# Issuing the attention scores of two heads together, alternating between the halves of the array's rows

## The chip, the cores and the metric

One core of a Trainium2 chip runs the whole program. The metric is the device time of one execution in microseconds (us); the median over several executions counts. The engines named below are PE (TensorE, the matrix products; its weight loads are listed apart as PEld), DVE (VectorE), ACT (ScalarE), POOL (GpSimd) and SP (SyncE, which issues the transfers).

## The reference

A backbone of two layers over 1024 latent tokens on a grid of 16 x 64 and 256 context tokens, 1024 channels, all in float32. The change lies in the neighbourhood attention of the first layer: 8 heads of 64 channels. A latent token attends to a window of 8 x 16 grid neighbours and to all context tokens; a context token attends to the context alone.

```python
s_nb = jnp.einsum('bchd,bicjhd->bhcij', q_row, k_nb) * scale + jnp.transpose(bias, (0, 2, 1, 3))
s_cx = jnp.einsum('bchd,bnhd->bhcn', q_row, k_ctx) * scale
p = jax.nn.softmax(jnp.concatenate([s_nb.reshape(n_b, n_h, GRID_W, n_win), s_cx], axis=-1), axis=-1)
...
return jnp.einsum('bhcij,bicjhd->bchd', p_nb, v_nb) + jnp.einsum('bhcn,bnhd->bchd', p[..., n_win:], v_ctx)
```

## The kernel before

The program runs through the layers in turn: projections of layer 0, then a stage in which attention and the mLSTM heads are made together, the output product, the MLP, and layer 1 (RWKV-7 and its MLP). The change touches only the stage of attention and mLSTM.

Heads lie in pairs: head 0 of a pair has its 64 channels on partitions 0 to 63 of the tiles q and k, head 1 on partitions 64 to 127. A product that contracts over 64 partitions uses the half of the array's rows that these partitions feed; the profile writes its form as 64\*128. The generator `attn_tiles` yields 80 tiles: for each of 4 pairs, for each of 10 blocks j of 128 queries (8 latent blocks, 2 context blocks), one tile for head 0 and then one for head 1. A tile with a neighbourhood has two score products: `s2`, against 256 context keys, and `s1`, against 384 neighbourhood keys (256 in the blocks at the left and right edge). A tile of a context block has `s2` alone. Each float32 product shows as two passes in the trace: 80 `s2` are 160 MATMUL records.

`attention` works on a tile in three steps, some tiles in flight. `first` issues the scores (L798, L803), takes the row minimum of `s2` on DVE (L799; q is negated), adds the bias to `s1` and takes the minimum on DVE (L804), then exponentials on ACT (L806 reads `s2`, L808). `second`, LA = 2 tiles later, transposes the probabilities on PE (L819, `ptr`) and copies them out on ACT or, each third time, DVE (L826, L824). `third`, one tile later, multiplies with the values (L836, `po`). Every product goes into one of 8 PSUM banks that the whole program shares under one tag (`kk.bank`); a bank comes back when its last reader is done.

`weave` advances four generators in turn: per attention tile two steps of the mLSTM heads (L667 `pc`, L683 and L685 `pa`, read by DVE L670 and L688 and ACT L687; at a head's start L646 `st` and L655 `kt`), 0.9 step of the modulation vectors (L151 `ada`, whose weights `araw` of 512 KB come by transfer), and now and then a load. A scheduler then sets each engine's order from this program order and gives out the banks; each engine runs its list in order. The SP list is one such list too, so a transfer waits for the ones ahead of it.

Of the kernel before, what the change touches and what calls it, by code (L numbers as in the profile page):

```python
# [33 lines left out]
def behind(gen, n):  # L34
    """The items of gen, each only after n more have come."""
    q = []
    for x in gen:
        q.append(x)
        if len(q) > n:
            yield q.pop(0)  # L40
    yield from q


def weave(*gens):
    """Advance (generator, steps per round, rounds of delay) in turn until all are done."""
    live = [[g, n, -n * d] for g, n, d in gens]
    while live:
        for e in list(live):
            e[2] += e[1]
            while e[2] >= 1:  # L50
                e[2] -= 1
                try:
                    next(e[0])
                except StopIteration:
                    live.remove(e)
                    break


class K:
    """Pools: W weights, S slabs, T small tiles, ps PSUM, cst constants, dram scratch."""  # L60
# [36 lines left out]
    def load_w(self, src, kt, n, eng=None, rows=128):  # L97
        """src [rows, kt, n] in DRAM -> exact parts (hi, lo), [rows, kt, n]."""
# [5 lines left out]
    def mmk(self, outs, w, x, cks, first, last):  # L104
        """One contraction tile of a product in three passes: outs[i] += w.T x over the chunks; w, x: (hi, lo)."""
# [12 lines left out]
def joint(kk, ws, xs, cks, name):  # L118
    """Products over the same operands (a list or a generator), by contraction tiles: banks of each."""
    ps = [[kk.bank(name) for _ in cks] for _ in ws]  # L120
    for k, x in enumerate(xs):
        for p, w in zip(ps, ws):
            kk.mmk(p, (w[0][:, k, :], w[1][:, k, :]), x, cks, k == 0, k == KC - 1)
    return ps


def ada_steps(kk, l, ada_w, blocks, raw, sb, ahead=1):
    """Modulation vectors of layer l, one block of 512 in five steps.  raw(): tile [128, 1024] for weights, loaded ahead; sb(): [128, 512]."""
# [14 lines left out]
    for i, (nb, q) in enumerate(todo):  # L143
# [19 lines left out]
        if nb in (2, 3, 8, 9):  # L163
            nc.vector.tensor_scalar(m, m, 1.0, None, ALU.add)      # parts 1 and 4 are kept as 1 + scale
# [3 lines left out]
def ada_w(kk, l, w, blocks, tags=("araw",)):  # L168
    """The same, with tiles of pool W."""
# [9 lines left out]
class Stats:  # L179
    """1 / rms over the channels of 8 slabs [128, n] that come one by one.  The tokens lie in 4 groups of n / 4, a quadrant of  # L180
    partitions each."""
# [14 lines left out]
    def rstd(self):  # L196
        """The result on all partitions: slab [128, n]."""
# [19 lines left out]
def norm_mod(kk, xt, n, mods, part, hs, segs, rstd):  # L217
    """Modulated rms norm, as exact parts hs[c] = (hi, lo); parts part (shift), part + 1 (1 + scale)."""
# [13 lines left out]
def mlp(kk, xt, n, hs, w1, w2, gate, segs, side=None, done=None):  # L232
    """xt += gate * relu(h w1)^2 w2, in place.  w1 [32, 128, 8, 128], w2 [32, 128, 1, 1024].  side: generator advanced along the way;
    done(c): called as xt[c] is complete."""
# [19 lines left out]
    def square(f):  # L254
        """relu(h w1)^2 as exact parts, a chunk a step."""
# [64 lines left out]
def out_proj(kk, w, rows, xt, n, mods, part, segs, ww):  # L320
    """xt += gate * (cat w), in place; ww: the weights of the first tiles, made together from the rows of cat as they come."""
# [33 lines left out]
NA = 12      # blocks of modulation vectors made beside attention and mLSTM  # L355
HD, AD = 9, 20
LA = 2
# [10 lines left out]
def proj_tokens(kk, hs, w, n, cb, tiles, rows):  # L368
    """Token-major products: cb(t, psum [128, n]) for each token tile.  w: (hi, lo) [128, 4, n] for each half of k."""
# [14 lines left out]
def mlstm_rows(kk, psg, I):  # L384
    """Gates -> quantities of each token, direction and head.  On partitions (direction, 16 chunks of which 10 are used, head): the
    tokens of a chunk; the running maximum passes from chunk to chunk on a second layout, partitions (direction, head).  A generator,
    then kk.mcols: M in DRAM [128, 128] and columns [128 t, 5, 2, 16, 4]: g, M_start - M_t, -m_t, g - M_end, M_start - M_end
    (exponentials but for g)."""
# [23 lines left out]
    # log sigmoid(f) = min(f, 0) - log1p(e), e = exp(-|f|); log1p(e) = 2 atanh(s), s = e / (2 + e)  # L412
# [94 lines left out]
def project0(kk, I, hs, dr, early):  # L507
    """Projections of layer 0, left in DRAM: qk (mLSTM, roped, channel-major), vb, sig(o), q and k (neighbourhood, channel-major,
    (column block, row, column) order), va (token-major, same order)."""
# [37 lines left out]
    # neighbourhood q, k by head pairs  # L547
# [71 lines left out]
def mlstm_head(kk, h, dr, cat):  # L619
    """One head, both directions; leaves the gated, normed output channel-major in DRAM."""  # L620
# [112 lines left out]
def attn_tiles(kk, I, dr):  # L733
    """The attention tiles: (start, finish stages) in order."""
# [50 lines left out]
def attention(kk, tiles):  # L785
    """Neighbourhood and context attention, some tiles in flight."""
# [3 lines left out]
    def first(tile):  # L790
        (q, knb, kcx, bias, vt), cell, x = tile[:3]         # q is negated: the scores come out as -s
# [5 lines left out]
        s2 = kk.bank("s2")  # L797
        nc.tensor.matmul(s2[:, 0:256], q, kcx, start=True, stop=True)  # L798
        V.tensor_reduce(m[:, 0:1], s2[:, 0:256], AX.X, ALU.min)  # L799
        mm = m[:, 0:1]  # L800
        if nb:
            s1 = kk.bank("s1")
            nc.tensor.matmul(s1[:, 0:nb], q, knb, start=True, stop=True)  # L803
            V.tensor_tensor_reduce(p[:, 0:nb], s1[:, 0:nb], bias, 1.0, m[:, 0:1], ALU.add, ALU.min, m[:, 1:2])  # L804
            mm = m[:, 1:2]
        nc.scalar.activation(p[:, nb:nb + 256], s2[:, 0:256], AF.Exp, scale=-1.0, bias=mm, accum_out=m[:, 2:3])  # L806
# [35 lines left out]
    for tile in tiles:  # L842
        if ends:
            drain(ends.pop())
        a1.append(first(tile))
        if a2:
            third(a2.pop(0))
        if len(a1) > LA:
            a2.append(second(a1.pop(0)))
        yield  # L850
# [18 lines left out]
def heads(kk, dr, cat):  # L869
    """The mLSTM heads, the end of each woven into the next."""  # L870
# [14 lines left out]
def load_wo(kk, w):  # L885
    """The weights of the first two tiles of the output product."""
# [10 lines left out]
def layer0(kk, I, mods, ada0):  # L897
    """The mixer of layer 0, up to the input of the output product: slabs of pool kk.CT."""
# [44 lines left out]
def out0(kk, I, xt, cat, mods):  # L943
    """xt += gate * (cat w_out), in place; cat is taken apart."""
    with kk.tc.tile_pool(name="O", reuse_waits="tile", bufs=8) as S:
        kk.S, kk.slab_w = S, NT
        parts = []
        for t in cat:
            hi, lo = kk.slab(NT, F32R, "ch"), kk.slab(NT, F32R, "cl", kk.CT)      # lo: in the room of the slab before
# [9 lines left out]
def mlp_layer(kk, xt, n, mods, w1, w2, segs, stats, side=None, done=None):  # L959
    """stats: of the rows of xt."""  # L960
# [18 lines left out]
# Tokens (context, latents).  Rows of h are padded: context at 1, latents at 258, zeros at 0, 257, 1282.  # L979
PIECES = ((0, 256, 1), (256, 768, 258), (768, 1280, 770))      # columns and where they start in the padded rows  # L980
# [3 lines left out]
def norm_h(kk, xt, mods, h, rstd):  # L984
    """Modulated rms norm of the stream (latents first), a chunk of channels a step; xt is taken apart.  A generator."""
# [16 lines left out]
def mix_piece(kk, C, h, c, s, q, w, hi, lo, eng):  # L1002
    """Exact parts of h + mu (S / 2 - h) for stream s, S = h[t - 1] + h[t + 1]: w columns from padded column q."""
# [10 lines left out]
class Stream:  # L1014
    """The mixed stream s in slabs, made a chunk of channels a step."""
# [19 lines left out]
def weights(kk, src):  # L1035
    """Exact parts of src [128, 8, n], in halves."""
# [3 lines left out]
def wide(kk, src, rows=128):  # L1040
    """Exact parts of src [rows, 1, 1024], in halves."""
# [7 lines left out]
def mm3(kk, outs, w, x, first, last):  # L1049
    """One contraction tile in three passes; outs: (psum, columns of x, whether its first product clears the bank)."""  # L1050
# [5 lines left out]
def pair_banks(kk, cks):  # L1056
    """PSUM of two products at once; their last chunks share a bank."""
# [12 lines left out]
def product(kk, w, st, cks, cb, after):  # L1070
    """cb(p, outs) for each of the 8 output tiles; st: the stream; after: called as a slab of the stream is done.  A generator, a
    step a contraction tile."""
# [26 lines left out]
def by_piece(d, i, a, b):  # L1099
    """Columns a..b of array i of a [5, 128, arrays, 256] tensor in DRAM."""  # L1100
# [7 lines left out]
def low_rank(kk, C, I, h, dr, X):  # L1108
    """g, the decay and the first product of a.  A generator; X: the operands of the second products."""
# [74 lines left out]
def second(kk, w2, x, p):  # L1184
    """A second product, operands [hi; lo] on the partitions."""
# [10 lines left out]
def knorm(kk, C, dr, rn):  # L1196
    """1 / |k k_k| of each head and token, as exact parts: rows 32 (p % 4) + 2 (p // 4) + head."""
# [21 lines left out]
def rwkv_proj(kk, I, h, norm, C, dr, free_h):  # L1219
    """Leaves in DRAM: k, a, r by pieces of 256 tokens (kar), sums of the decay's sigmoid from a token to the middle of its span of 128 and sigmoid(a) of both  # L1220
    directions (css), v (token-major), g (channel-major)."""
# [62 lines left out]
    # r, with the second product of a, a itself and the coefficients of the bonus: sum r k (2 + k_a (sa_f + sa_b - 2)) r_k  # L1284
# [64 lines left out]
T = 12              # steps of the schedule from one item to the next  # L1349
# [13 lines left out]
class Unit:  # L1363
    """A pair of heads in one direction."""
# [5 lines left out]
class Item:  # L1370
    """A piece of 4 chunks of 64 tokens of a unit."""
# [6 lines left out]
class Batch:  # L1378
    """Items whose triangular blocks are inverted together, 16 partitions an item."""
# [16 lines left out]
def item_a(kk, C, dr, it, nxt):  # L1396
    """Decayed operands, their products and the transposed keys.  In the backward direction A and B are in reversed order of time."""
# [3 lines left out]
    # E, EI: exponentials of the decay's sum to the middle of the span of two chunks, at the token itself (own) and at its neighbour  # L1401
    # (nb).  wl: factors of the state as it enters the first and the second span, and E at the end of the second
# [678 lines left out]
```

## Time and profile before

| | us |
|---|---|
| median of 3 runs | 4408.41 (4404.98 to 4411.24) |
| span of the profiled execution, first to last instruction | 4413.2 |
| stage of attention and mLSTM, first score to last attention output | 503 to 867, so 364 |
| PE busy in that stage | 345.9 |
| DVE busy, ACT busy in that stage | 215.6, 209.1 |

The profiled execution is 4.8 us (0.1%) longer than the median of the timed runs. Durations are taken from it, and differences worked out from it are applied to the median. A timeline row gives start, duration, engine, line and form; several alike are merged with their count, and their duration runs from the first start to the last end. Since passes of PE overlap in their pipeline, the time that a pass occupies PE is read from start to start.

### The profile page before, as it was taken

Reading aid. Unit: us, or ns where it says so; the run is one execution under the profiler, and the core shown is the slowest. Engines: PE = TensorE matmul, PEld = TensorE weight load, DVE = VectorE, ACT = ScalarE, POOL = GpSimd, SP = SyncE. Lnnn points to the kernel's source line nnn. Section 1 sums busy time; section 2 is a strip of 40 time slices with the busy share of each in tenths; the row PEclk is TensorE's granted clock in tenths of the full one; section 3 lists DMA queues with packets and bytes.
Section 4 is the critical chain, followed back from the end, with each engine's and each line's share of the span. In section 5 each row is a group of like instructions: output and inputs, shape, how many; then the busy total and the mean of one; then the engine's idle time right before and its main releaser. Section 6 shows DMA issues by size and latency. Waiting matters only on the chain. (4 is left out here: it accounts for less than half of the span.)

```text
span 4413.2 us, 71606 instructions
## 1 busy us (share of the span) xinstructions
PE 4159.4 (94%) x27565; PEld 3345.2 (76%) x27565; DVE 2578.8 (58%) x4890; ACT 1693.4 (38%) x4095; POOL 1303.3 (30%) x1530
## 2 busy tenths in 40 slices
PE   6999998998999999997979986999999998999999
PEld 3899876676777888874757765888888865888887
DVE  4320366517556666669684436777777535666666
ACT  4142455513111111125655444666666532111111
POOL 4111010024111111116533344455555223222221
PEclk9999999999999999998979997999999998999999
DMA  4414345411222111111343554444444331111111
GB/s 171 118 62 137 91 142 141 172 47 34 86 82 64 37 39 39 35 59 54 100 126 101 175 176 105 114 123 130 131 130 126 82 134 40 51 48 48 48 48 62
DMA packets 389185, 409.15 MB, mean 93 GB/s; under 512 B 149884, under 2 KB 305820, under 8 KB 388844
## 3 DMA queue, kind: packets, MB, share of 16 engines
q1 hardware_dynamic: 388844, 404.58, 30.7%
q8 instruction: 217, 3.56, 0.3%
q14 instruction: 124, 1.02, 0.1%
HBM read 304.71 MB, written 95.57 MB: 91 GB/s over the span
## 5 line engine op out<-in xcount | busy, mean ns | idle before, releaser
L280 DVE SCALAR_TENSOR_TENSOR x<-m,mods,x 128x512 f32<-128x512 f32 x1280 | 823.6, 690 | 571.1 <-PE m L110 570.9
L95 POOL TENSOR_TENSOR wl<-raw,wh 128x1024 fp32r<-128x1024 f32 (+1 forms) x236 | 510.0, 2164 | 1913.0 <-ACT wh L94 1874.0
L94 ACT ACTIVATE wh<-raw 128x1024 fp32r<-128x1024 f32 (+1 forms) x236 | 221.5, 940 | 1363.4 <-PE m L110 1065.0
L110 PE MATMUL m<-h,wh 128*128 128x512 f32 (+1 forms) x2560 | 633.2, 375 | 25.5 <-POOL h L229 17.9
L110 PEld LDWEIGHTS m<-h,wh 128*128 128x128 f32 x2560 | 451.0, 189 | 148.1 <-POOL h L229 27.7
L110 PE MATMUL m<-hidh,wh 128*128 128x512 f32 x1280 | 357.2, 372 | 3.5 <-DVE x L280 3.5
L110 PE MATMUL m<-hidl,wh 128*128 128x512 f32 x1280 | 355.0, 370 | 0.8 <-DVE hidl L267 0.7
L110 PE MATMUL m<-h,wl 128*128 128x512 f32 x1280 | 353.2, 372 | 0.0
L110 PE MATMUL m<-hidh,wl 128*128 128x512 f32 x1280 | 352.3, 370 | 0.0
L377 PE MATMUL pt<-wh,h 128*128 128x256 f32 x1600 | 289.3, 283 | 0.0
L110 PEld LDWEIGHTS m<-hidh,wh 128*128 128x128 f32 x1280 | 224.0, 188 | 54.2 <-DVE x L280 11.5
L110 PEld LDWEIGHTS m<-hidl,wh 128*128 128x128 f32 x1280 | 224.4, 188 | 44.5 <-DVE hidl L267 2.2
L110 PEld LDWEIGHTS m<-h,wl 128*128 128x128 f32 x1280 | 225.3, 189 | 42.5
L110 PEld LDWEIGHTS m<-hidh,wl 128*128 128x128 f32 x1280 | 224.0, 188 | 42.8 <-issue 0.5
L377 PEld LDWEIGHTS pt<-wh,h 128*128 128x128 f32 x1600 | 250.0, 192 | 0.0
L1449 PE MATMUL G<-AR,BZ 128*128 128x128 f32 x1280 | 231.5, 306 | 19.1 <-POOL EI L1420 6.2
L377 PE MATMUL pt<-wl,h 128*128 128x256 f32 x800 | 226.4, 283 | 0.0
L1486 DVE TENSOR_TENSOR prd<-P,R 80x31 f32<-80x31 f32 (+15 forms) x496 | 205.5, 414 | 22.8 <-DMA P<-ga 10.3
L1487 DVE TENSOR_TENSOR R<-R,prd 80x31 f32<-80x31 f32 (+15 forms) x496 | 206.3, 416 | 6.9
L1449 PEld LDWEIGHTS G<-AR,BZ 128*128 128x128 f32 x1280 | 176.4, 200 | 42.5 <-POOL EI L1420 7.0
L1006 POOL TENSOR_TENSOR ss<-h 128x512 f32<-128x512 f32 (+1 forms) x128 | 154.0, 1213 | 122.3 <-DVE xt L1009 97.9
L1452 DVE TENSOR_TENSOR G<-G,c_gmask 128x512 f32<-128x512 f32 (+1 forms) x160 | 101.1, 634 | 141.6 <-PE G L1449 141.6
(408 smaller groups left out, 8379.4 us busy)
## 6 DMA issues: line engine op xcount, KB each, us to landing
raw<-in_w SPq DMA_DIRECT2D x128, 512.0 KB
araw<-in_ada_w SPq DMA_DIRECT2D x80, 512.0 KB
kar<-rw_kar SPq DMA_DIRECT2D x64, 384.0 KB
css<-rw_css SPq DMA_DIRECT2D x80, 256.0 KB
x<-in_xT SPq DMA_DIRECT2D x16, 640.0 KB
raw<-in_w_v SPq DMA_DIRECT2D x20, 512.0 KB
rw_css<-rs SPq DMA_DIRECT2D x16, 640.0 KB
UV<-rw_v SPq DMA_DIRECT2D x80, 128.0 KB
```

The costliest lines, as they stand in the source:

```text
L94: self.nc.scalar.activation(hi, raw, AF.Copy)
L95: (eng or self.nc.gpsimd).tensor_tensor(lo, raw, hi.bitcast(F32), ALU.subtract)
L110: mm(o[:M, :b - a], ww, xx[:, a:b], start=(first and p == 0), stop=(last and p == 2))
L280: V.scalar_tensor_tensor(xt[c][:, u:v], p[:, u - a:v - a], gate[:, c, cond:cond + 1], xt[c][:, u:v], ALU.mult, ALU.add)
L377: mm(ps[:, :n], xx[:, sl], ww[:, k % 4, :], start=(k == 0 and p == 0), stop=(k == KC - 1 and p == 2))
L1006: nc.gpsimd.tensor_tensor(S, h[:, q - 1:q - 1 + w], h[:, q + 1:q + 1 + w], ALU.add)
L1449: nc.tensor.matmul(ps[:, 128 * j:128 * j + 128], BZ[h][:, j, :], AR[:, j, :], start=True, stop=True)
L1452: V.tensor_tensor(G[:, :, h, 0:m], ps.rearrange("q (c t) -> q c t", t=128)[:, :, 0:m], mask[:, :, 0:m], ALU.mult)
L1486: V.tensor_tensor(pr, P3[:, s, s + 1:32].unsqueeze(1).to_broadcast([n_, w, n]), R3[:, 0:w, s].unsqueeze(2).to_broadcast([n_, w, n]), ALU.mult)
L1487: V.tensor_tensor(R3[:, 0:w, s + 1:32], R3[:, 0:w, s + 1:32], pr, ALU.add)
```

## The change

`first` no longer issues scores. A new function `scores` takes a pair of tiles, head 0 and head 1 of the same query block, and issues `s2` of head 0, `s2` of head 1, `s1` of head 0, `s1` of head 1. The loop of `attention` takes two tiles at a time, issues their scores, and then goes through the two tiles as before. Softmax, transposes, value products and the interleaving with the other generators keep their program order; docstrings and comments that the diff also removes are not shown.

```diff
-    def first(tile):
-        (q, knb, kcx, bias, vt), cell, x = tile[:3]         # q is negated: the scores come out as -s
+    def scores(pair):
+
+        out = [[None, None] for _ in pair]
+        for kind in (1, 0):
+            for o, tile in zip(out, pair):
+                q, knb, kcx = tile[0][:3]
+                k = kcx if kind else knb
+                if k is not None:
+                    o[kind] = kk.bank("s2" if kind else "s1")[:, :k.shape[1]]
+                    nc.tensor.matmul(o[kind], q, k, start=True, stop=True)
+        return out
+
+    def first(tile, s1, s2):
+        (q, knb, kcx, bias, vt), cell, x = tile[:3]
...
-        s2 = kk.bank("s2")
-        nc.tensor.matmul(s2[:, 0:256], q, kcx, start=True, stop=True)
-        V.tensor_reduce(m[:, 0:1], s2[:, 0:256], AX.X, ALU.min)
+        V.tensor_reduce(m[:, 0:1], s2, AX.X, ALU.min)
...
-            s1 = kk.bank("s1")
-            nc.tensor.matmul(s1[:, 0:nb], q, knb, start=True, stop=True)
-            V.tensor_tensor_reduce(p[:, 0:nb], s1[:, 0:nb], bias, 1.0, m[:, 0:1], ALU.add, ALU.min, m[:, 1:2])
+            V.tensor_tensor_reduce(p[:, 0:nb], s1, bias, 1.0, m[:, 0:1], ALU.add, ALU.min, m[:, 1:2])
...
     for tile in tiles:
-        if ends:
-            drain(ends.pop())
-        a1.append(first(tile))
-        if a2:
-            third(a2.pop(0))
-        if len(a1) > LA:
-            a2.append(second(a1.pop(0)))
-        yield
+        pair = [tile, next(tiles)]
+        sc = scores(pair)
+        for i in range(2):
+            if ends:
+                drain(ends.pop())
+            a1.append(first(pair[i], *sc[i]))
+            sc[i] = None
+            if a2:
+                third(a2.pop(0))
+            if len(a1) > LA:
+                a2.append(second(a1.pop(0)))
+            yield
```

Outside the stage no engine's order changes. Inside it, 33 of the 40 pairs have all their score products in one piece on PE's list (8 of them are the pairs of context blocks, which have two products); in 7 pairs one or more other products stand between them.

On PE, the list of before at the start of the stage: two edge tiles of head 0 and head 1 (256 neighbourhood keys each), then the first tile of the next block. The scores of the first three tiles follow each other with nothing between.

```order
L798 MATMUL s_4749<-aq 128x256
L803 MATMUL s_4752<-aq 128x256
L798 MATMUL s_4761<-aq 128x256
L803 MATMUL s_4764<-aq 128x256
L798 MATMUL s_4773<-aq 128x256
L803 MATMUL s_4776<-aq 128x384
```

Here head 0 issues both its products before head 1 issues its first. After the change the list begins with two pairs.

```order
L799 MATMUL s_4746<-aq 128x256
L799 MATMUL s_4748<-aq 128x256
L799 MATMUL s_4750<-aq 128x256
L799 MATMUL s_4752<-aq 128x256
L799 MATMUL s_4771<-aq 128x256
L799 MATMUL s_4773<-aq 128x256
L799 MATMUL s_4775<-aq 128x384
L799 MATMUL s_4777<-aq 128x384
```

The heads of a pair now alternate, and the fourth tile has come forward to stand with the third.

On PE in the middle of the stage, before: one tile from its scores to the scores of the next.

```order
L798 MATMUL s_6145<-aq 128x256
L803 MATMUL s_6148<-aq 128x384
L836 MATMUL po<-va,ptsb 128x64 x5
L819 MATMUL ptr<-ident,ap 128x128 x5
L667 MATMUL pc<-vb,kw 128x129
L683 MATMUL pa<-vb,mb 128x129
L685 MATMUL pa<-cst,qT 128x129
L667 MATMUL pc<-vb,kw 128x129
L683 MATMUL pa<-vb,mb 128x129
L685 MATMUL pa<-cst,qT 128x129
L151 MATMUL ada<-araw,cs 32x512 x2
L798 MATMUL s_6200<-aq 128x256
```

The next tile's scores come 10 rows after this tile's. The same place after: four products of the pair, then what followed one tile, and the same again for the second tile without any scores ahead of it.

```order
L799 MATMUL s_6143<-aq 128x256
L799 MATMUL s_6145<-aq 128x256
L799 MATMUL s_6147<-aq 128x384
L799 MATMUL s_6149<-aq 128x384
L844 MATMUL po<-va,ptsb 128x64 x5
L827 MATMUL ptr<-ident,ap 128x128 x5
L667 MATMUL pc<-vb,kw 128x129
L683 MATMUL pa<-vb,mb 128x129
L685 MATMUL pa<-cst,qT 128x129
L667 MATMUL pc<-vb,kw 128x129
L683 MATMUL pa<-vb,mb 128x129
L685 MATMUL pa<-cst,qT 128x129
```

The scores of the second tile have moved forward by one tile, to stand with those of the first. On DVE at that place after the change: the scheduler puts the minima of both tiles and then the bias steps of both tiles behind each other (L809, L812 are L799, L804 of before), ahead of the copy and of the mLSTM steps; before, one minimum and one bias step stood between two groups of mLSTM steps.

```order
L809 TENSOR_REDUCE am<-s_6143 128x1
L809 TENSOR_REDUCE am<-s_6145 128x1
L812 ISA ap,am<-s_6147,bias,am 128x384
L812 ISA am 128x1
L812 ISA ap,am<-s_6149,bias,am 128x384
L812 ISA am 128x1
L832 COPY ptsb<-ptr 128x512
L818 RECIPROCAL arc<-am 128x1
L670 SCALAR_TENSOR_TENSOR cst<-cst,mcols,pc 128x129 x2
L818 RECIPROCAL arc<-am 128x1
```

The second tile's minimum and bias step have come forward by one tile, as its scores have on PE.

## Rows read from the trace of the kernel before

**Rows 1.** The page's first line.

```profile
span 4413.2 us, 71606 instructions
```

**Rows 2.** Stretches: us, busy time of PE, PEld, DVE, ACT, POOL, clock, DMA.

```profile
503.00:867.00 364.00, 345.91 (x2163) 247.66 (x2162) 215.55 (x658) 209.11 (x635) 35.37 (x76) 0.96 0.49 141
```

**Rows 3.** Groups by form on PE, 503 to 867: busy us, mean ns.

```profile
L798 PE MATMUL s<-aq 64*128 64x256 f32 x160 | 54.9, 427 | 0.0
...
L803 PE MATMUL s<-aq 64*128 64x384 f32 x96 | 39.9, 496 | 0.0
...
L803 PE MATMUL s<-aq 64*128 64x256 f32 x32 | 9.0, 379 | 0.2 <-ACT kw L657 0.2
```

**Rows 4.** Timeline of PE around a tile with 384 neighbourhood keys.

```profile
629.02 0.60 PE L776 MATMUL pot<-ident,ao 128*128 128x128 f32 x4
629.55 0.70 PE L798 MATMUL s<-aq 64*128 64x256 f32 x2
...
630.82 1.33 PE L836 MATMUL po<-va,ptsb 128*128 128x64 f32 x10
631.98 0.71 PE L819 MATMUL ptr<-ident,ap 128*128 128x128 f32 x5
632.53 0.28 PE L667 MATMUL pc<-vb,kw 128*128 128x129 f32 x1
```

**Rows 5.** Timeline of PE at an edge tile and a context tile.

```profile
546.36 0.70 PE L798 MATMUL s<-aq 64*128 64x256 f32 x2
...
547.42 0.43 PE L836 MATMUL po<-va,ptsb 128*128 128x64 f32 x2
...
554.78 0.70 PE L798 MATMUL s<-aq 64*128 64x256 f32 x2
555.41 0.43 PE L836 MATMUL po<-va,ptsb 128*128 128x64 f32 x2
```

**Rows 6.** Timeline of PE at the start of the stage.

```profile
503.04 0.71 PE L798 MATMUL s<-aq 64*128 64x256 f32 x4
503.57 0.60 PE L803 MATMUL s<-aq 64*128 64x256 f32 x4
504.01 0.59 PE L798 MATMUL s<-aq 64*128 64x256 f32 x2
504.44 0.81 PE L803 MATMUL s<-aq 64*128 64x384 f32 x2
```

**Rows 7.** Timeline of PE, DVE and ACT through the softmax of one tile.

```profile
704.66 0.70 PE L798 MATMUL s<-aq 64*128 64x256 f32 x2
...
705.39 0.42 DVE L799 TENSOR_REDUCE am<-s 128x1 f32<-128x256 f32 x1 [1.63 <-PE s L798]
...
706.13 0.61 DVE L804 CUSTOM_DVE_ANT_0 ap<-s,bias,am 128x384 f32<-128x384 f32 x1
...
706.78 0.47 ACT L806 ACTIVATE ap<-s,am 128x256 f32<-128x256 f32 x1 [2.57 <-DVE am L804]
...
707.10 0.72 PE L819 MATMUL ptr<-ident,ap 128*128 128x128 f32 x5
...
707.25 0.60 ACT L808 ACTIVATE ap<-ap,am 128x384 f32<-128x384 f32 x1
...
707.65 0.39 PE L667 MATMUL pc<-vb,kw 128*128 128x129 f32 x2
707.74 0.69 DVE L824 COPY ptsb<-ptr 128x512 f32<-128x512 f32 x1 [0.99 <-PE ptr L819]
...
708.32 0.39 PE L667 MATMUL pc<-vb,kw 128*128 128x129 f32 x2
```

**Rows 8.** PE's waits in 503 to 867: us in total, times, longest.

```profile
PE ada L151 <- DMA araw<-in_ada_w: 9.4, 2, 5.5
PE kt L655 <- DVE am L804: 3.0, 1, 3.0
```

**Rows 9.** Timeline of SP and of PE around one such wait.

```profile
573.74 0.38 SPq L631 DMA_DIRECT2D vb<-l_vb  x1
...
592.15 1.92 PE L151 MATMUL ada<-araw,cs 128*32 128x512 f32 x4 [3.85 <-DMA araw<-in_ada_w]
```

More of the change, by code (lines that the diff above doesn't have):

```diff
@@ L796, in first @@
         p = kk.tmp([128, 640], "ap", bufs=LA + 2)
-        s2 = kk.bank("s2")
-        nc.tensor.matmul(s2[:, 0:256], q, kcx, start=True, stop=True)
-        V.tensor_reduce(m[:, 0:1], s2[:, 0:256], AX.X, ALU.min)
+        V.tensor_reduce(m[:, 0:1], s2, AX.X, ALU.min)
         mm = m[:, 0:1]
         if nb:
-            s1 = kk.bank("s1")
-            nc.tensor.matmul(s1[:, 0:nb], q, knb, start=True, stop=True)
-            V.tensor_tensor_reduce(p[:, 0:nb], s1[:, 0:nb], bias, 1.0, m[:, 0:1], ALU.add, ALU.min, m[:, 1:2])
+            V.tensor_tensor_reduce(p[:, 0:nb], s1, bias, 1.0, m[:, 0:1], ALU.add, ALU.min, m[:, 1:2])
             mm = m[:, 1:2]
-        nc.scalar.activation(p[:, nb:nb + 256], s2[:, 0:256], AF.Exp, scale=-1.0, bias=mm, accum_out=m[:, 2:3])
+        nc.scalar.activation(p[:, nb:nb + 256], s2, AF.Exp, scale=-1.0, bias=mm, accum_out=m[:, 2:3])
         if nb:
```

## The prediction

> **What bounds the kernel now.** I read the span first, 4413.2 us [rows 1], and then only the stage that the change touches, since no engine's order changes outside it. In the stage's 364 us PE is busy 345.91, DVE 215.55 and ACT 209.11 [rows 2]: PE has 95% of the time, the others under 60%. So time taken from PE there is time taken from the stage, as long as nothing else ends later. PE's waits say what is left: 9.4 us in two waits for weights of the modulation product and 3.0 us at the start of an mLSTM head, where DVE is named [rows 8]; nothing notable is waited for at the scores themselves. The groups by form give the counts [rows 3]: at two passes a product, 160 records are 80 tiles with `s2`, 96 are 48 tiles with 384 neighbourhood keys, 32 are 16 edge tiles, and 80 - 64 = 16 tiles have `s2` alone. Their mean durations (427, 496, 379 ns) hold pipeline overlap, so I don't multiply them, but read the occupancy from start to start.
>
> **What a tile's scores cost.** From the first score to the next other product: 630.82 - 629.55 = 1.27 us for a 384 tile [rows 4]; 547.42 - 546.36 = 1.06 for an edge tile and 555.41 - 554.78 = 0.63 for a context tile [rows 5]. Entering costs a little more: five transposes take 632.53 - 631.98 = 0.55, so 0.11 each, but the four transposes ahead of the scores take 629.55 - 629.02 = 0.53 instead of 0.44 [rows 4]. These 0.09 us come with every switch from the full array to a half. All tiles: 48 x 1.36 + 16 x 1.15 + 16 x 0.72 = 95.2 us of PE in the stage.
>
> **What two heads together cost.** Before has one place where two tiles of different halves follow each other with nothing between, the start of the stage. There four passes of `s2`, two tiles of them, start at 503.04 and the `s1` group starts at 503.57, 0.53 us later, lasting to 504.01, 0.44 us [rows 6]. A single tile's `s2` right behind takes 504.44 - 504.01 = 0.43 for two passes [rows 6]. So four passes of two halves take as long as two passes of one. What is more, `s2` of head 1 ran beside `s2` of head 0 although `s1` of head 0 stands between them on the list (the order of before in the section on the change): each half works its own list off, and neither waits for the other.
>
> The Trainium skill ("TensorE: Matmul & The Clock Gate", part 3 on packing small matmuls) says that tiles on different rows overlap, but that matmuls start and end strictly in program order. On the overlap the trace agrees; on the order it does not, since by that rule the second `s2` could not have started with the first. What the rule would make of the time is a rival below.
>
> **The sum.** With both halves busy, a pair costs what one tile costs, so half of 95.2 us goes: 47.6. From it:
> - The first pair (edge tiles) overlaps already: 1.15 us less. Left 46.4.
> - Seven pairs have other products between their scores. Such a pair still overlaps in part and pays an entry more; bounds are nothing saved and everything saved (1.36 us each, so 9.5 us or nothing lost). I take half, 4.6 us. Left 41.8.
> - Two waits of 3.85 and 5.50 us are for weights behind a burst of transfers, and the 3.0 us at an mLSTM head's start [rows 8, 9] stands at such a burst too. The wait at 592.15 began at 588.3, and its burst at 573.74 [rows 9]. Where the transfers set the end, what PE saves in between is only waited for later: 14.6 us of PE's work, at 364 / 80 = 4.55 us a tile about 3.2 tiles, each 0.68 us shorter: 2.2 us a place, three places: 6.6 us given back. If the bursts moved earlier by the same amount, nothing would be. Left 35.
> - Banks and DVE, the only new wait. Four of 8 banks now hold scores; `po` and the modulation product hold one each; two are free. I replay one pair by hand with the durations of one tile [rows 7], from the first score. DVE's minimum starts 705.39 - 704.66 = 0.73 later and takes 0.42, so the two end at 1.15 and 1.57. The bias step to ACT's start takes 706.78 - 706.13 = 0.65: done at 2.22 and 2.87, which frees the `s1` banks. ACT's first exponential takes 0.47, and ACT needs 707.25 + 0.60 - 706.78 = 1.07 a tile: `s2` of head 0 is free at 2.69, of head 1 at 3.76. PE meanwhile: scores to 1.27, `po` takes 631.98 - 630.82 = 1.16 [rows 4], to 2.43, `ptr` into the two free banks to 2.98. Then `pc`, `pa`, `pc`, `pa` need a bank each, and a step takes 708.32 - 707.65 = 0.67 [rows 7]: at 2.98, 3.20, 3.65 and 3.87. The banks come at 2.22, 2.87, 2.69 and, for the fourth, 3.76 (the copy of `ptr` ends at 2.43 + 707.74 + 0.69 - 707.10 = 3.76 too). So each is in time, the last by 0.1 us only. In the second half of the pair four more are free. Bounds: nothing, or the rival below. A margin of 0.1 will not hold everywhere; I take 0.1 us for each of the 32 pairs with a neighbourhood: 3.2 us. Left about 32.
>
> What the change adds elsewhere costs nothing: DVE and ACT do the same operations, at 59% and 57% of the stage's time now and about 65% in a stage of 332 us. SP's list has a few neighbours exchanged (a load of keys or values ahead of a weight load); 0.5 us to issue [rows 9], inside the term of the bursts.
>
> By differences from the profiled span the stage goes from 364 to 332 and the span from 4413.2 to 4381.2; the timed median is 4.8 us below the span, so 4408.4 - 32 = 4376 us.
>
> **Rivals.**
> 1. *Passes start in list order.* A product is two passes; in order, head 1's first pass starts with head 0's second, and so on: five pass times for eight. A 384 pair then takes four starts of 0.32, 0.22, 0.32 and 0.32 us, an end of 0.41 and the entry, 1.68 in all, and saves 1.04 instead of 1.36; an edge pair saves 0.93, a context pair 0.50: 24 x 1.04 + 8 x 0.93 + 8 x 0.50 = 36.4 (the 0.22, 0.32 and the ends are from [rows 4 to 6]: 0.43 / 2 for 256 columns, half as much again for 384, 0.09 for the first pass and the last). With the other terms in proportion: 36.4 - 0.9 - 3.5 - 6.6 - 3.2 = 22 us, 4386. Against it stand [rows 6].
> 2. *Transfers take more.* If all of the stage's waits for transfers grow, not at three places but at each head's start and for the weights in between, half of the gain goes: 4392. For it: transfers are 0.49 of the DMA time [rows 2], in bursts, and SP's list blocks behind loads that wait for a free tile. Against it: only three places wait now [rows 8].
> 3. *Banks.* The fourth `pa` must wait whenever DVE or ACT is late, since the last bank of the pair's scores comes at 3.76. If DVE has 1.0 us of mLSTM work ahead of the minimum, PE stands for 0.9 us, and the 32 pairs give back 29 of 35 us: 4402, no change to speak of. If PE waits 1.6 us, for both exponentials of the second tile and the copies behind them on ACT's list, the stage is longer by 32 x 1.6 - 35 = 16 us: 4424, slower. It decides at 35 / 32 = 1.1 us a pair. For it: DVE now has 2.1 us of softmax in one piece ahead of the mLSTM steps. Against it: DVE idles 1.63 us before the minimum in [rows 7], so it is not late at that place.
>
> The Trainium skill warns of this one ("TensorEngine Tiling (Array Packing)", restrictions and gotchas): row tiling raises PSUM pressure, since row tiles need banks of their own. The order shows that each of the four products has its own bank; what the pressure costs no row of before shows.
>
> **How the numbers follow.** My forecast, a gain of 20 to 46 us with 32 as the likeliest, has 0.65; rival 1 has 0.09 and rival 2 0.11 (both faster); rival 3 with no change has 0.10 and slower 0.05. A gain over 0.2% is one of 9 us, about what a measurement of this kernel can tell from no change: faster 0.85, same 0.10, slower 0.05. Range: the low end is a gain of 46, all of the sum but the first pair, 4362; the high end takes in rivals 1 and 2, 4398.
>
> **What would show it.** In the changed trace `s` should come as eight passes in about 1.3 us where a tile took 1.27, and the sum of all scores from start to start should fall from 94 (95.2 less the first pair's 1.15) to about 52 us (47.6 and 4.6). The stage from first score to last attention output should take about 332 us. If PE shows new idle time before `pa`, `pc` or `ptr` with DVE or ACT named, rival 3 has come; if the waits for `araw` grow well past 9.4 + 6.6 us, rival 2; if eight passes take 1.6 us, rival 1. The prediction is wrong if halves don't run beside each other away from the start of the stage, or if bank waits exceed some 0.3 us a pair.

## The result and the profile after

The changed kernel takes 4384.0 us against 4411.2 for the kernel before (7 runs each): ratio 0.9936, 95% interval 0.9917 to 0.9956. A second series gave 4388.6 against 4410.7, ratio 0.9933 (0.9908 to 0.9958). So it is faster by 22 to 27 us, where 32 was the forecast and 4362 to 4398 the range.

The first two lines of the page after, beside [rows 1]:

```profile
span 4389.3 us, 71617 instructions
...
PE 4121.9 (94%) x27565; PEld 3323.6 (76%) x27565; DVE 2576.4 (59%) x4890; ACT 1690.6 (39%) x4095; POOL 1300.2 (30%) x1530
```

Stretches of the kernel after: us, busy time of PE, PEld, DVE, ACT, POOL, granted clock, DMA share. The first is the whole stage, as [rows 2] for before, the others its beginning.

```profile
503.00:845.00 342.00, 313.69 (x2169) 230.53 (x2168) 210.23 (x658) 206.56 (x635) 36.23 (x76) 0.96 0.50 151
...
503.00:512.00 9.00, 6.11 (x38) 4.80 (x37) 4.13 (x17) 5.08 (x18) 0.82 (x5) 0.83 0.68 223
512.00:520.00 8.00, 8.00 (x45) 5.84 (x44) 3.60 (x12) 3.57 (x11) 0.39 (x2) 0.77 0.99 257
520.00:530.00 10.00, 9.76 (x78) 8.12 (x76) 6.94 (x26) 7.01 (x24) 0.77 (x4) 1.00 0.62 224
```

The stage has gone from 364 to 342 us. PE is busy 32.2 us less (313.69 for 345.91 in [rows 2]), but idle 28.3 instead of 18.1: it has lost 10 us more to standing. Now PE and ACT on the timeline after, at the start of the stage and a little later:

```profile
503.63 2.21 PE L799 MATMUL s<-aq 64*128 64x256 f32 x16
...
506.66 0.66 PE L827 MATMUL ptr<-ident,ap 128*128 128x128 f32 x4 [0.82 <-ACT ap L816]
...
508.15 0.60 ACT L816 ACTIVATE ap<-ap,am 128x384 f32<-128x384 f32 x1
...
508.75 0.58 ACT L834 ACTIVATE ptsb<-ptr 128x512 f32<-128x512 f32 x1
...
509.39 1.97 PE L844 MATMUL po<-va,ptsb 128*128 128x64 f32 x8 [2.08 <-ACT ptsb L834]
...
512.14 2.51 PE L799 MATMUL s<-aq 64*128 64x256 f32 x8
514.58 1.63 PE L844 MATMUL po<-va,ptsb 128*128 128x64 f32 x8
...
524.17 1.35 PE L799 MATMUL s<-aq 64*128 64x256 f32 x8
525.45 1.33 PE L844 MATMUL po<-va,ptsb 128*128 128x64 f32 x10
```

At 524.17 eight passes, four of them over 384 keys, occupy PE for 525.45 - 524.17 = 1.28 us; one tile's four passes took 1.27 [rows 4]. That is the gain, as forecast. The rows above it show a cost: at the start the scores of four tiles are out by 506, PE then waits 0.82 us for an exponential and 2.08 for a copy of probabilities that ACT makes only at 508.75, behind the exponentials of three tiles. After that the granted clock is 0.77 from 512 to 520 (full is 2.4 GHz, 0.50 is 1.2), and the same eight passes at 512.14 take 514.58 - 512.14 = 2.44 us. Before, PE had the full clock there:

```profile
512.00:520.00 8.00, 8.00 (x50) 5.74 (x48) 3.22 (x13) 4.26 (x15) 0.58 (x3) 1.00 1.15 233
```

PE's waits in the stage after, beside [rows 8]: us in total, times, longest.

```profile
PE ada L151 <- DMA araw<-in_ada_w: 6.4, 2, 5.9
PE ptr L827 <- DVE am L812: 5.1, 1, 5.1
PE po L844 <- ACT ptsb L834: 3.8, 3, 2.1
PE kt L655 <- ACT ptsb L834: 3.1, 1, 3.1
PE pa L683 <- DVE am L812: 3.0, 2, 1.9
```

The waits for `kt` and `ptr` stand at the starts of mLSTM heads, the second and the fourth of four. On the timeline of DVE and PE there:

```profile
588.54 1.66 DVE L648 SCALAR_TENSOR_TENSOR mb<-mb,mcols,c_mx 128x128 f32<-128x128 f32 x6 [4.29 <-DMA mb<-mrows]
590.14 0.33 PE L655 MATMUL kt<-ident,kT 128*128 128x128 f32 x1 [3.10 <-ACT ptsb L834]
...
731.94 0.61 DVE L648 SCALAR_TENSOR_TENSOR mb<-mb,mcols,c_mx 128x128 f32<-128x128 f32 x2 [5.67 <-DMA mb<-mrows]
732.47 0.61 DVE L812 CUSTOM_DVE_ANT_0 ap<-s,bias,am 128x384 f32<-128x384 f32 x1
733.15 0.48 PE L827 MATMUL ptr<-ident,ap 128*128 128x128 f32 x1 [5.12 <-DVE am L812]
```

At the fourth head DVE waits 5.67 us for a transfer of rows (`mb`, made in L636 and L637) that opens a head, its bias step (L812) stands behind that on its list, and PE behind the bias step. At the second head DVE waits 4.29 us for rows, and PE waits for a copy that ACT makes behind the step that follows those rows. Before, two waits stood behind rows, the 3.0 us for `kt` in [rows 8] and this one:

```profile
PE ptr L819 <- ACT ap L806: 1.4, 1, 1.4
```

The two waits for `pa` have another cause: the bias step stands still until GpSimd has negated a bias tile (L750).

**The balance.** To set these against each other I divide the time from the first score pass to the first pass of the output product. Scores: from the start of each score pass to PE's next start, at most 0.414 us (what the last pass of a 384 tile takes at full clock). Rest: all else, divided at the 57th pass with the values (`po`), about 24 us into the stage. All from the start times of PE's records. At the low clock the longest passes take more than 0.414 us; what is over counts as rest.

| us | whole | scores | rest, to the 57th value pass | rest behind it |
|---|---|---|---|---|
| before | 368.4 | 87.6 | 11.9 | 268.9 |
| after | 345.6 | 50.5 | 17.6 | 277.4 |
| after, second profile (below) | 343.9 | 50.7 | 16.3 | 277.0 |

So the scores give 37 us, and 14.3 or 12.4 are given back: 5.8 or 4.4 at the start and 8.5 or 8.0 later.

### The profile page after: what moved, and what is told of

It is laid out like the page before. It is cut to its first block, busy times and chain, and to the rows that moved or that the text cites. A ratio compares the mean times of both kernels' runs of the same rounds, so it can differ in the third digit from the quotient of the medians.

```text
span 4389.3 us, 71617 instructions
## 1 busy us (share of the span) xinstructions
PE 4121.9 (94%) x27565; PEld 3323.6 (76%) x27565; DVE 2576.4 (59%) x4890; ACT 1690.6 (39%) x4095; POOL 1300.2 (30%) x1530
```

## The experiments

Each time below is from the first score pass to the first pass of the output product, unless it says otherwise; four numbers in a row are those of the table.

**Where the gain comes from.** Scores issued in pairs, but of two query blocks of one head, so in one half of the array:

```diff
-            for j in js:
-                for hp in range(2):
+            for jp in js[::2]:
+                for hp, j in ((0, jp), (0, jp + 1), (1, jp), (1, jp + 1)):
```

> Pairs are formed of two query blocks of the same head, so both tiles of a pair lie in the same half of the array's rows; everything else is as in the changed kernel. Theory (the gain comes from the two halves running beside each other; issuing pairs costs some 18 us elsewhere in the stage): scores save only the switches, about 0.28 us a pair, so they take about 83 us from start to start instead of 94 before and 53 after; the stage is 5 to 12 us longer than before, the ratio to before about 1.002. Rival (the gain comes from issuing four products in a piece): as the changed kernel, ratio 0.994, stage about 346 us.

Ratio to before 0.9997 (0.9977 to 1.0018); 373.2, 82.9, 22.8, 267.5. The saving on scores is 4.7 us and not 37, so nearly all of it needs the two halves. Here, too, the start is dear, 22.8 for 11.9 us, and its stretches show why:

```profile
512.00:520.00 8.00, 8.00 (x25) 5.61 (x25) 2.56 (x8) 1.76 (x5) 0.19 (x1) 0.50 0.89 239
520.00:530.00 10.00, 10.00 (x33) 7.03 (x31) 2.53 (x9) 3.29 (x10) 0.39 (x2) 0.50 0.26 79
```

PE is busy all the time, at 0.50 of the clock. Behind the start the rest is 1.4 us under before: pairs cost nothing there as long as PE gets no faster. That speaks for PE's being faster as the cause of what the change gives back later, and for the pairs as the cause of what it gives back at the start.

The same pair, but both products of head 0 ahead of both of head 1, by exchanging two loops in `scores`:

```diff
-        for kind in (1, 0):
-            for o, tile in zip(out, pair):
+        for o, tile in zip(out, pair):
+            for kind in (1, 0):
```

> The pair's four products are issued together, but head 0 issues both of its products before head 1 does. Theory (each half works off its own list, so the order between halves does not matter): eight passes in about 1.28 us as in the changed kernel, scores about 53 us in all, ratio about 0.994. Rival (matmuls start in list order): only the end of head 0 overlaps the start of head 1, a 384 pair takes about 2.1 us, scores about 80 us in all, ratio about 1.000.

Ratio 0.9937 (0.9915 to 0.9959); 344.8, 53.7, 17.2, 274.0. The first sixteen passes:

```profile
504.06 2.31 PE L799 MATMUL s<-aq 64*128 64x256 f32 x16
```

They take 2.31 us where the alternating order takes 2.21 and eight passes in one half, then eight in the other, 3.18 (the run before this one):

```profile
504.30 3.18 PE L799 MATMUL s<-aq 64*128 64x256 f32 x16
```

So the alternation that the change writes is hardly needed: over the stage the scores take 53.7 us for 50.5, and the stage is no longer. A half takes its next product from behind two products of the other half, as at the start of the stage before [rows 6]. With four ahead it did not: in the first 0.9 us of the same-half run, where four products of one half come first, only four passes have started, and eight in the head-by-head run.

```profile
504.30 1.13 PE L799 MATMUL s<-aq 64*128 64x256 f32 x4
...
504.06 1.14 PE L799 MATMUL s<-aq 64*128 64x256 f32 x8
```

What sets this reach no run here shows. By the rule of the Trainium skill ("TensorE: Matmul & The Clock Gate", part 3, what overlaps and what doesn't), matmuls start and end in program order; then head by head only the middle passes of a pair could overlap. The trace of the head-by-head run does not agree.

**Is it given back at the modulation weights?** Both kernels with 47 of the stage's 48 loads of these weights left out (the first tile is used again in their place):

```diff
-        if i < len(todo):
+        if once:
+            ws.append(once[0])
+        elif i < len(todo):
...
             ws.append(w)
+            if once is not None:
+                once.append(w)
```

> The kernel before, with one load of modulation weights in the stage instead of 48: the other 47 loads (24 MB) are left out and the products use the one tile, so the modulation vectors are not the reference's. It is the control for the next run. Theory (stops at the starts of mLSTM heads wait for transfers that queue behind these weights): the stops of 3.9, 5.5 and 3.0 us shrink to under half, the stage is 8 to 16 us shorter than 368.4. Rival (the stops come from elsewhere): within 4 us of 368.4.

> The changed kernel with the same 47 loads left out. Theory (what the change gave back, it gave back at transfers): the stage is 28 us or more shorter than that of the control, against 22.8 us between the changed kernel and the kernel before. Rival (it was given back at ACT, DVE and banks): the difference to the control stays 20 to 25 us.

Before with this edit: ratio 0.9989 (0.9967 to 1.0011); 358.1, 87.5, 11.9, 258.7. After with it: 0.9927 (0.9899 to 0.9955); 339.6, 50.4, 19.3, 269.9. The control is 10.3 us shorter than before, as forecast. The difference between the two is 18.5 us, not larger but smaller than 22.8: the weights do not take the gain, and this theory falls; the rival's 20 to 25 us is missed too. What holds PE instead:

```profile
PE kt L659 <- ACT kw L661: 16.3, 10, 5.9
PE po L848 <- ACT ptsb L838: 2.2, 2, 2.1
```

The same wait has 6.2 us in the control. It stands at the heads' starts, where DVE waits for the rows (15.9 us in six waits, 13.8 in the control). With the weights gone the faster PE stands the more at the rows.

**Is it the rows behind other loads?** Both kernels with a head's rows issued ahead of its values and gates:

```diff
-    vb = kk.slab(1300, F32, "vb").rearrange("p (c e) -> p c e", e=130)
...
-    sg = kk.slab(NT, F32, "sg")
...
     es = []
     for d in range(2):
         mb = kk.slab(NT, F32, "mb")
...
         es.append(mb)
+    vb = kk.slab(1300, F32, "vb").rearrange("p (c e) -> p c e", e=130)
...
+    sg = kk.slab(NT, F32, "sg")
...
```

> The kernel before, with the rows of an mLSTM head (the broadcast that DVE's first step of a head waits for, 3.9 to 4.6 us at three head starts) issued ahead of that head's values and gates instead of behind them. Theory that this transfer sets PE's stops at the heads: values and gates are 1.28 MB, some 4 us at the rate of about 300 GB/s that the stretch shows, so the three DVE waits fall to 0 to 2 us each, PE's stops (3.85, 5.50 and 3.03 us) lose 5 to 9 us together, and the stretch from the first score pass to the first output product goes from 368.4 to 360 to 363 us; ratio to the kernel before about 0.998. Rival, that values or modulation weights, now later on the list, hold PE at the same places: 366 to 370 us, ratio 0.999 to 1.001.

> The changed kernel with the same edit, the rows of an mLSTM head issued ahead of its values and gates. Theory that what the change saves between head starts is partly waited for at the rows: DVE's three waits (3.3 to 5.7 us) fall to 0 to 2, PE's stops there (14 us together) lose 6 to 10 us, the stretch goes from 344 to 345.6 to 335 to 339 us, the ratio to the kernel before to 0.990 to 0.992, and the stretch is shorter than that of the kernel before with the same edit by 25 to 28 us, more than the 22.8 to 24.5 between the unedited ones. Rival, that these stops cost both kernels alike or that values and weights take the rows' place: a difference of 22 to 25 us, and a stretch of 342 to 346 us in the second case.

Before with this edit: ratio 0.9993 (0.9972 to 1.0015); 370.6, 87.9, 12.4, 270.4. After with it: 0.9978 (0.9961 to 0.9994); 366.2, 54.7, 26.9, 284.6. The theory falls in both kernels: DVE waits for the rows as long as without the edit. In the changed kernel it was 16.6 us in all; with the rows first it is

```profile
DVE mb L648 <- DMA mb<-mrows: 17.7, 5, 5.8
```

Yet the loads ahead did delay the rows. At the fourth head the changed kernel issues the first load at 714.77, and the second tile of rows is there at 731.9, 17.1 us later (the wait above); with the rows first it takes from 736.25 to 749.8, 13.5 us. The first line is of the changed kernel, the others of the edited one:

```profile
714.77 0.37 SPq L631 DMA_DIRECT2D vb<-l_vb  x1
...
736.25 1.08 SPq L632 DMA_DIRECT2D mb<-mrows  x2
...
743.75 2.19 DVE L648 SCALAR_TENSOR_TENSOR mb<-mb,mcols,c_mx 128x128 f32<-128x128 f32 x8 [1.88 <-DMA mb<-mrows]
...
749.89 0.61 DVE L648 SCALAR_TENSOR_TENSOR mb<-mb,mcols,c_mx 128x128 f32<-128x128 f32 x2 [3.95 <-DMA mb<-mrows]
```

At the second and third head it is 13.0 for 16.7 and 14.0 for 17.4 us. But DVE comes to its step sooner as well, at these three heads 7.4, 8.2 and 9.7 us behind the first load instead of 12.5, 12.9 and 11.5: the edit also moved the step on DVE's list (at the third head 38 tiles' minima stand ahead of it, not 40). And a head's two tiles of rows land some 6 us apart in both kernels, so the second is late even from the head of the list. The experiment therefore does not tell what earlier rows alone would give.

The length of the changed kernel's stage was in no theory: nearly all of the change's gain is gone. It goes to the clock and not to waits. Over the whole stage PE is busy 333.5 us for 313.7 in the changed kernel, idle 29.5 for 28.3, and the granted clock is 0.90 for 0.96:

```profile
503.00:866.00 363.00, 333.52 (x2172) 246.27 (x2170) 211.42 (x658) 207.06 (x635) 33.88 (x76) 0.90 0.46 143
```

Half of the loss is at the start, in the stretches of this kernel:

```profile
503.00:512.00 9.00, 6.11 (x42) 4.97 (x40) 4.12 (x17) 5.07 (x18) 0.77 (x4) 0.89 0.67 235
512.00:520.00 8.00, 8.00 (x31) 5.46 (x29) 2.68 (x8) 3.57 (x11) 0.43 (x3) 0.50 0.70 136
520.00:530.00 10.00, 10.00 (x38) 7.93 (x38) 4.61 (x16) 3.55 (x13) 0.38 (x2) 0.50 1.01 315
530.00:540.00 10.00, 10.00 (x41) 8.34 (x40) 5.05 (x19) 3.15 (x12) 0.40 (x2) 0.50 0.02 5
```

PE stands for the same 2.9 us as in the changed kernel (6.11 us busy in the first 9), then works through to 540 without a gap and at half the clock. Its list up to there is that of the changed kernel but for one score product in another place. The 112th value pass is done 57.0 us into the stage, 45.3 in the changed kernel: 11.7 us. Another 7 are lost by the 252nd pass, around a wait of 5.6 us at the second head, with the clock at 0.70 from 590 to 620.

**Is it banks?** Both kernels with one PSUM bank held through the stage, by a product whose reader comes after it:

```diff
+        hold = kk.bank("hold")
+        nc.tensor.matmul(hold[:, 0:128], kk.ident, kk.ident, start=True, stop=True)
...
+        nc.vector.tensor_copy(kk.tmp([128, 4], "am", bufs=LA + 4), hold[:, 0:4])
```

> The kernel before, with one PSUM bank held by an idle tile through the stage, so 7 banks go round; control for the next run. Both theories: little, the stage is 0 to 3 us longer than 368.4.

> The changed kernel with one bank held, so 7 go round. If banks are what the change gives time back for (rival 3 of the prediction, the margin of 0.1 us in the replay), one bank less makes every pair wait 0.2 to 0.5 us: the stage is 6 to 16 us longer than 345.6 and PE shows waits at pa, pc and ptr with DVE or ACT named. If banks have slack, it stays within 4 us.

Before with seven banks: ratio 1.0053 (1.0026 to 1.008); 378.0, 88.6, 11.9, 277.6. After with seven: 0.997 (0.9957 to 0.9983); 354.5, 54.7, 17.2, 282.6. I had expected the first to lose 3 us at most; it loses 9.6, the changed kernel 8.9. The timed ratios say more, 23 us (11 to 35) and about 15 us; what lies beyond the profiled stages is not shown. Banks are scarcer than I read, but in both kernels, and a bank less does not eat the gain (23.5 us between the two stages).

**Can the start be mended, and a later stop?** The first three pairs tile by tile as before:

```diff
+        one = done < NS1
+        done += 1
-        sc = scores(pair)
+        sc = [None, None] if one else scores(pair)
         for i in range(2):
+            if one:
+                sc[i] = scores(pair[i:i + 1])[0]
```

> The first three pairs issue their scores tile by tile, as before the change; from the fourth pair on as in the changed kernel. Theory (at the start of the stage two pairs of scores come at once, the exponentials of four tiles stand on ACT ahead of the copies that PE waits for, PE idles 2.9 us and loses its clock until about 519): the first value product comes about 1.5 us earlier, the clock stays at 1.00, and the stage is 3 to 5 us shorter than the changed kernel's 345.6. Rival (the start waits for the transfers and loads that begin there): the idle time stays and the stage keeps its length within 2 us.

Ratio 0.9941 (0.992 to 0.9961); 345.1, 52.5, 12.9, 279.8. On PE's timeline the first pass with the values now comes 4.83 us behind the first score pass, without a wait, where it took 5.76:

```profile
503.22 2.20 PE L800 MATMUL s<-aq 64*128 64x256 f32 x12
...
508.05 1.11 PE L845 MATMUL po<-va,ptsb 128*128 128x64 f32 x8
```

The granted clock stays at 1.00, and the start costs 4.7 us less (3.4 less than in the second profile of the change, below). But the stage is as long as without the edit: scores cost 2 us more (three pairs no longer overlap), and the rest behind the start 2.4. The start's loss is real, and mending it yields nothing that can be seen.

In the first profile after, PE also stood 1.86 us at 772 for a bias step that waited for GpSimd's negation of a bias tile (L750). With that negation on VectorE:

```diff
-            nc.gpsimd.tensor_scalar(bt, bt, -1.0, None, ALU.mult)
+            nc.vector.tensor_scalar(bt, bt, -1.0, None, ALU.mult)
```

> The sign change of the two bias tiles of a head pair is moved from POOL (2.4 us a tile) to DVE. Theory (after the change both heads' bias is needed at once, so the second bias tile, ready only after two POOL operations, stops DVE's bias step, keeps a score bank and stops PE at pa): the stop of 1.9 us near 772 and a smaller one near 569 go, the stage is 3 to 6 us shorter than the changed kernel's 345.6. Rival (the bias transfer itself is late): DVE now stands for the transfer, the stage keeps its length or grows by up to 5 us.

Ratio 0.9937 (0.9914 to 0.996); 342.3, 49.9, 17.7, 274.7, and the stop is gone. I took that for 3.3 us gained, until the next two runs. Both edits together:

> This is the changed kernel with two edits at once: the first three pairs of the stage keep their score passes tile by tile (from the fourth pair on both tiles go out together), and the negation of the bias tiles is done by VectorE instead of GpSimd. Theory that the two stops are separate and what they cost is really saved: alone the first edit left the stretch from the first score pass to the first output product at 345.1 us (345.6 in the changed kernel) and the second at 342.3; together they should give 341 to 342, a span of 4384 to 4387 and a ratio to the kernel before of 0.992 to 0.994. Rival, that the stage is held elsewhere and what is saved early is waited for again at the next stop: 344 to 346 us, with longer waits for DVE's bias step or for the arriving modulation weights, and a ratio of 0.993 to 0.995. The sizes lie close together, so the stretch in the profile decides and not the time.

and the changed kernel itself once more:

> The changed kernel itself once more, beside the version with both edits on the same chip. It tells how far the length of the stage scatters from one profiled execution to another: if the 345.6 us from the first score pass to the first output product come again within 1 us, differences of 3 us between kernels can be read from single profiles; if they come out 2 us or more apart, the edits that moved the stage by 0.5 and 3.3 us are not told from the changed kernel. Ratio to the kernel before 0.991 to 0.996.

Both edits: 4383.2 us, ratio 0.9923 (0.99 to 0.9946); 344.2, 52.0, 12.9, 279.4. The change again (time and ratio stand above as the second series): 343.9, 50.7, 16.3, 277.0. The second profile of one and the same kernel is shorter by 1.7 us, and its stretch around that stop (between the 449th and the 505th value pass) by 2.9, 42.0 for 44.9, without any edit. The two edits do not add up, and the rival has it: PE's wait for `ptr` behind DVE's bias step is 9.8 us with both edits,

```profile
PE ptr L828 <- DVE am L813: 9.8, 2, 5.0
```

9.3 with the bias edit alone, and 5.1 without. The wait that is added stands at the second head, where the rows come late. There the changed kernel waits 3.7 us (0.57 for `ptr`, 3.10 for `kt`), with the first pairs tile by tile 5.0, with the bias edit 5.9 and with both 5.9. So a good part of what is saved ahead of this head is waited for at it. No version is shown to beat the change.

## Why the prediction was right, and where its sum was off

**The halves overlap: right.** Eight passes take 1.28 us (about 1.3 was forecast), and the scores from start to start, uncapped, went from 93.65 to 52.96 (94 and 52). The term was 47.6 - 1.15 - 4.6 = 41.8 us. In the table's terms 33 x 0.09 = 3.0 of it, entries that fall away, lie in the rest, and 38.8 in the scores; measured are 37.1 and 36.9.

**What is given back: mis-sized.** The step that failed is "Banks and DVE, the only new wait", 3.2 us, which with the 6.6 at transfers makes 9.8, less the 3.0 of entries 6.8 us in the rest. Measured are 14.3 and 12.4. Behind the start it is 8.5 and 8.0, near enough in size, but not for the reason given: the replay had each of 32 pairs wait 0.1 us for its last bank, and what stands in the traces is a few long stops. The start's 5.8 and 4.4 us were not in the sum at all. I replayed a pair from the middle of the stage, where `po` and `ptr` of earlier tiles keep PE busy while DVE and ACT work. At the start there are no earlier tiles, and the order in the section on the change shows it: four tiles' scores in a row. ACT has three tiles' exponentials ahead of the first copy, PE stands for 2.9 us, and the clock does the rest. That pairing does this is shown from both sides: all eight profiles with pairs at the start spend 16.3 to 26.9 us of rest there and show the clock below full, the two with only the first three pairs tile by tile 12.9, and the four that go tile by tile throughout 11.9 to 12.4, at the full clock. How much of the later 8 us is transfers and how much the softmax I can't divide: the waits that stand at transfers and heads (`ada`, `kt` and `ptr` behind `am` or `ptsb`) grew from 12.4 to 14.6 us, by 2.2 where 6.6 was the forecast, and those for `pa` from 0.5 to 3.0 (1.6 in the second profile). These last stand behind the bias tiles, which a pair now needs both at once; the sum had no term for them. Nor do the places add up as causes: with the start mended the stage was no shorter, so the start's part can't be taken for a gain that was there to be had.

**The rivals.** Passes in list order: refuted, by 1.28 us a pair and by the head-by-head order. Transfers take more: not as the rival had it, for PE's waits for `araw` fell from 9.4 to 6.4 us, and without those loads the gain is no larger; but the waits behind rows grew, from 4.4 us (`kt` 3.0, `ptr` 1.4) to 8.2 for `ptr` and `kt` alone. Banks: no, though the sign that was set for it showed: waits for `pa`, `pc` and `ptr` with DVE or ACT named come to 10.5 us (8.6 in the second profile) for 2.7 before, some 0.3 us a pair. But 5.1 of them stand behind rows and 3.0 behind bias tiles, one bank less costs both kernels 9 us of the stage, and nowhere does PE stand 1.1 us a pair.

**The sum.** 32 us were forecast for the stage and 22.8 and 24.5 came: 7.5 to 9.2 short, of which 1.7 to 1.9 are scores, 4.4 to 5.8 the start and 1.2 to 1.7 later. The spans fell by 23.9 and 30.9 us; of the second, 5.6 us lie behind the stage, where the order of no engine differs. So the timed 27 us of the first series, nearer to the forecast than the stage is, should not be read as a better sum: the second series gives 22.

## What to carry to other kernels

Products that use half of the array's rows should stand next to products of the other half on the list; the order within the pair mattered little here (3 us of scores, nothing in the stage). A replay of one step from the middle must be made again for the first steps of the stage, where nothing earlier covers the latency, and a stop there is priced with the low clock that may follow it, even where mending it, as here, brings nothing. When the bounding engine gets faster, part of the saving is waited for further on (here 8 of 37 us), and one kernel is profiled twice before 2 to 3 us are read from a pair of profiles.

## What the runs showed of the hardware that was not expected

- Each half of the rows starts its next product ahead of list order, within limits: in the head-by-head order the sixteen passes take 2.31 us for 2.21, though two products of head 0 stand ahead of head 1's first. With four ahead they take 3.18, so the prediction's "neither waits for the other" goes too far.
- After one and the same stop of 2.9 us the clock stayed low for very different times: in 512 to 520 it was 1.00 in the second profile of the change and 0.77 in the first, and with the rows first 0.50 up to 540, PE busy throughout. Over its stage that kernel had PE busy 20 us longer. The Trainium skill ("TensorE: Matmul & The Clock Gate", part 1) says that the number of products at the low clock differs between runs of one kernel; the two profiles of the change agree. Why the kernel with the rows first stays low so long no run here settles.
- One of eight PSUM banks less made the profiled stage 9.6 us longer before the change and 8.9 after it; in the timed ratios it is 23 and about 15 us.
